# A 2x2 average pool: stores of one tile against stores of two tiles

## The chip, the cores and the metric

One core of one Trainium2 chip runs the kernel. The metric is the device time of one execution in microseconds, as a median over several runs; the profiled execution's *span* (first to last instruction) is some 1.8 us shorter. "Landing" is the moment when a DMA has signalled on all 16 engines that it is done.

## The reference

```python
# x: (32, 128, 256, 256) float32, kernel_size 2, stride 2 -> out: (32, 128, 128, 128) float32
for i in range(h_out):
    for j in range(w_out):
        output[:, :, i, j] = np.mean(x[:, :, 2*i:2*i+2, 2*j:2*j+2], axis=(2, 3))
```

1073.7 MB are read, 268.4 MB are written, each once.

## The kernel before

The output rows (32 x 128 x 128 of them, 128 floats each) are cut into tiles of 128 partitions x 32 rows. A tile's load is 64 KB per partition (8.4 MB), its store 16 KB per partition (2.1 MB). SP issues the loads, DVE adds rows and then columns, ACT multiplies by 0.25 and issues the stores. There are two input slots and two result slots in turn; a third result slot serves only the remainder at the end, which is loaded, summed and stored in pieces of 16, 8, 4 and 4 rows.

```python
    ins = [in_pool.tile([P, TILE, 2 * w], f32, name="in_tile") for _ in range(2)]
    res = [out_pool.tile([P, TILE, w_out], f32, name="res") for _ in range(3)]
    ...
    def take(engine, sem, n=1):           # wait for the semaphore, then take n off
        engine.wait_ge(sem, n)
        engine.sem_inc(sem, -n)
    def load(t, b):
        sp.dma_start(out=ins[b], in_=xt[t]).then_inc(loaded[b], 16)
    def sums(it, dst):
        dve.tensor_add(out=it[:, :, 0:w], in0=it[:, :, 0:w], in1=it[:, :, w:]).then_inc(halfway)
        take(dve, halfway)
        dve.tensor_add(out=dst, in0=it[:, :, 0:w:2], in1=it[:, :, 1:w:2]).then_inc(summed)
    def tile_sums(b):
        take(dve, stored[b], 16)          # the store of tile t-2 has landed
        take(dve, loaded[b], 16)          # the load of tile t has landed
        sums(ins[b], res[b])
    def scale_store(t, b, landed):
        take(act, summed)
        act.sem_inc(free[b])              # SP may load tile t+2
        scale(res[b])
        take(act, scaled)
        act.dma_start(out=ot[t], in_=res[b]).then_inc(landed, 16)
    ...                                   # loops over 127 whole tiles, then the pieces
```

## Time and profile before

| | before |
|---|---|
| median of the first 3 runs | 3103.62 us (3103.59 to 3103.67) |
| span of the profiled run | 3101.5 us |
| rate of all bytes over the span | 433 GB/s |
| DVE, ACT busy | 54%, 15% |

The page gives the busy share of each engine, then the two DMA queues with packets, megabytes and the share of the 16 DMA engines' time that their packets took. In the timeline a line is start, duration, engine, source line, operation, output<-input; the bracket is the idle time before it. "SPq" and "ACTq" are sequencers that issue DMAs. The lines themselves stand in the prediction.

### The profile page before, as it was taken

The numbers are of one execution on the slowest core, as the hardware profiler recorded it, in microseconds if no ns is written. First come the engines' busy times: TensorE is split into PE (matmuls) and PEld (weight loads), VectorE is DVE, ScalarE is ACT, GpSimd is POOL, SyncE is SP. The second block draws the span as 40 slices with busy tenths as digits, with TensorE's granted clock in tenths as the row PEclk, the third lists the DMA queues.
The fourth block names the chain that finished last, engine by engine and source line by source line (L and its number), as shares of the span: only waits on it lengthen the run. The fifth ranks groups of instructions, "written<-read, shape, count | busy, mean of one in ns | idle before, by whom it ended". The sixth has DMA issues, their size and how long they took to land. (4 is left out here: it accounts for less than half of the span.)

```text
span 3101.5 us, 2614 instructions
## 1 busy us (share of the span) xinstructions
DVE 1679.6 (54%) x262; ACT 464.7 (15%) x132; POOL 0.2 (0%) x4
## 2 busy tenths in 40 slices
DVE  4555555555555555555555555555555555555556
ACT  1111111111111111111111111111111111111111
POOL 0000000000000000000000000000000000000000
DMA  9999999999999999999999999999999999999999
GB/s 416 436 440 426 436 440 426 437 440 424 438 440 423 439 437 425 440 428 434 440 433 430 442 423 436 439 427 440 435 426 437 439 427 436 438 424 439 437 425 416
DMA packets 37728, 1342.19 MB, mean 433 GB/s; under 512 B 4192, under 2 KB 4192, under 8 KB 4576
## 3 DMA queue, kind: packets, MB, share of 16 engines
q1 hardware_dynamic: 19008, 1075.85, 80.1%
q10 hardware_dynamic: 18720, 266.35, 20.1%
HBM read 1073.74 MB, written 268.44 MB: 433 GB/s over the span
## 5 line engine op out<-in xcount | busy, mean ns | idle before, releaser
L87 DVE TENSOR_TENSOR in_tile<-in_tile 128x8192 f32<-128x8192 f32 (+1 forms) x131 | 1113.0, 8496 | 1396.4 <-DVEq L67 1396.4
L97 ACT ACTIVATE res<-res 128x4096 f32<-128x4096 f32 (+1 forms) x131 | 463.5, 3538 | 2594.8 <-ACTq L67 2594.8
L89 DVE TENSOR_TENSOR res<-in_tile 128x4096 f32<-128x4096 f32 (+1 forms) x131 | 566.8, 4327 | 19.2
L97 ACT ACT_TABLE_LOAD x1 | 1.3, 1283 | 36.3 <-ACTq L67 36.3
L234 POOL MEMSET const-bfloat16-1.0<- 128x1 bf16 x1 | 0.1, 101 | 0.0
L234 POOL MEMSET const-uint8-127<- 128x1 uint8 x1 | 0.1, 101 | 0.0
L234 POOL MEMSET const-float32-0.0<- 128x1 f32 x1 | 0.1, 98 | 0.2 <-issue 0.2
L234 POOL MEMSET const-float32-1.0<- 128x1 f32 x1 | 0.1, 98 | 0.0
## 6 DMA issues: line engine op xcount, KB each, us to landing
out_dram<-res ACTq DMA_DIRECT2D x126, 2048.0 KB, 30.8
in_tile<-in_x_dram SPq DMA_DIRECT2D x1, 4096.0 KB, 22.0
in_tile<-in_x_dram SPq DMA_DIRECT2D x1, 2048.0 KB, 27.1
in_tile<-in_x_dram SPq DMA_DIRECT2D x2, 1024.0 KB, 30.0
out_dram<-res SPq DMA_DIRECT2D x1, 2048.0 KB, 11.7
in_tile<-in_x_dram SPq DMA_DIRECT2D x127, 31.5
out_dram<-res ACTq DMA_DIRECT2D x1, 1024.0 KB, 8.1
out_dram<-res ACTq DMA_DIRECT2D x1, 512.0 KB, 6.0
```

The source lines that it names most:

```text
L87: dve.tensor_add(out=it[:, :, 0:w], in0=it[:, :, 0:w], in1=it[:, :, w:]).then_inc(halfway)
L89: dve.tensor_add(out=dst, in0=it[:, :, 0:w:2], in1=it[:, :, 1:w:2]).then_inc(summed)
L97: act.mul(out=dst, in_=dst, mul=0.25).then_inc(done)
L234: nc = _bacc.Bacc("TRN2", target_bir_lowering=False, num_devices=1)
```

## The change

The intent: half as many store DMAs, each twice as large. The two result slots become two pairs, ACT issues one store per pair (two 16 KB pieces per partition, which lie 2 MB apart in HBM), and DVE waits for a store only at the first tile of a pair. This takes the third slot's room, so the remainder's result goes to the input slot that no load needs any more; the remainder has three pieces (16, 8, 8).

```diff
-    res = [out_pool.tile([P, TILE, w_out], f32, name="res") for _ in range(3)]
+    both = [out_pool.tile([P, 2, TILE, w_out], f32, name="res") for _ in range(2)]
+    res = [both[t // 2][:, t % 2] for t in range(4)]
...
+    op = ov[0:2 * pairs * TILE * P].rearrange("(k t p g) f -> k p t (g f)", t=2, p=P, g=TILE)
...
-        b = rest if rest - a <= 4 else a + (rest - a) // 2
+        b = rest if rest - a <= 8 else a + (rest - a) // 2
...
-    def tile_sums(b):
-        take(dve, stored[b], 16)
-        take(dve, loaded[b], 16)
-        sums(ins[b], res[b])
+    def tile_sums(t):
+        if t % 2 == 0:
+            take(dve, stored[t // 2 % 2], 16)
+        take(dve, loaded[t % 2], 16)
+        sums(ins[t % 2], res[t % 4])
...
-    def scale_store(t, b, landed):
-        take(act, summed)
-        act.sem_inc(free[b])
-        scale(res[b])
-        take(act, scaled)
-        act.dma_start(out=ot[t], in_=res[b]).then_inc(landed, 16)
+    def scale_store(pair, c, landed):
+        for b in range(2):
+            take(act, summed)
+            act.sem_inc(free[b])
+            scale(both[c][:, b])
+        take(act, scaled, 2)
+        act.dma_start(out=op[pair], in_=both[c].rearrange("p t g f -> p t (g f)")).then_inc(landed, 16)
...
-        it, dst = ins[whole % 2], res[2]
+        it = ins[whole % 2]
+        dst = ins[(whole + 1) % 2].rearrange("p g (s f) -> p (g s) f", s=4)[:, 0:TILE]
...                                       (loops regrouped to match; last waits adapted)
```

## The prediction

Passages that no trace or run of this case shows are cut from the prediction and from some expectations, at the marks. No term of the sum is among them: it stands as 3103.62 - 0.65 + 0.7 = 3103.7.

> **What bounds the kernel now.** I read the page first: busy shares, slices, DMA queues.
>
> ```profile
> span 3101.5 us, 2614 instructions
> DVE 1679.6 (54%) x262; ACT 464.7 (15%) x132; POOL 0.2 (0%) x4
> DMA  9999999999999999999999999999999999999999
> ...
> DMA packets 37728, 1342.19 MB, mean 433 GB/s; under 512 B 4192, under 2 KB 4192, under 8 KB 4576
> ...
> q1 hardware_dynamic: 19008, 1075.85, 80.1%
> q10 hardware_dynamic: 18720, 266.35, 20.1%
> ```
>
> No compute engine is near its limit; the 16 DMA engines are busy in every slice. q1 (loads, issued by SP) and q10 (stores, issued by ACT) take 80.1 + 20.1 = 100.2% of the engines' time: they are full, and packets even overlap a little. The bytes are given: 1073.7 MB in, 268.4 MB out. The chain of waits at the page's end tells nothing here (only the last scale is in it), so I went to the timeline, in the middle of the run:
>
> ```profile
> 1510.36 72.93 SPq L84 DMA_DIRECT2D in_tile<-in_x_dram  x4
> 1514.04 0.34 ACTq L104 DMA_DIRECT2D out_dram<-res  x1
> 1520.94 8.69 DVE L87 TENSOR_TENSOR in_tile<-in_tile 128x8192 f32<-128x8192 f32 x1 [10.93 <-DVEq L67]
> 1529.78 4.43 DVE L89 TENSOR_TENSOR res<-in_tile 128x4096 f32<-128x4096 f32 x1
> 1534.39 3.62 ACT L97 ACTIVATE res<-res 128x4096 f32<-128x4096 f32 x1 [20.58 <-ACTq L67]
> 1538.24 0.34 ACTq L104 DMA_DIRECT2D out_dram<-res  x1
> 1545.13 8.69 DVE L87 TENSOR_TENSOR in_tile<-in_tile 128x8192 f32<-128x8192 f32 x1 [10.93 <-DVEq L67]
> ```
>
> A tile takes 1545.13 - 1520.94 = 24.19 us, for 8.389 MB in and 2.097 MB out: 433.5 GB/s, the mean of the whole run. DVE needs 13.3 us of it and waits 10.9. What ends that wait is to be seen from the landings of the two issuing lines, loads first, then stores:
>
> ```profile
> DMA to landing us min/median/max: 21.8/31.5/40.7
> ...
> DMA to landing us min/median/max: 19.5/30.8/33.8
> ```
>
> The load issued at 1510.36 lands at about 1541.9; the store issued at 1514.04 lands at 1514.04 + 30.8 = 1544.8, and DVE starts at 1545.13. So DVE starts at the landing of the *store* of two tiles earlier, and the load lay ready for 3 us. This looks as if the store buffers bound the kernel, and is the trap of this profile: the store is slow only because the engines are full. When one store lands, the next is already queued (issued at 1538.24), and so is the next load (issued at about 1534.5). Neither queue runs dry, so an earlier start of DVE would only lengthen a queue.
>
> The last view is the DMA view of two short windows, from 24 to 34 us (loads alone) and from 1508 to 1520 us (both):
>
> ```profile
> q1 hardware_dynamic: 64, 4.19, 96.7%
> ...
> q1 hardware_dynamic: 80, 4.19, 80.7%
> q10 hardware_dynamic: 79, 1.05, 20.5%
> ```
>
> 64 load packets in 96.7% of 16 x 10 us are 2.42 us each, for 64 KB. In the second window 64 load packets and 16 tiny ones that end a load take 80.7% of 16 x 12 us; the window before it has the 64 alone at 80.6%. So the 16 tiny ones of a whole DMA cost 0.1% of 192 us, 0.2 us in all or about 0.01 us on each engine (rounding allows 0 to 0.02). The stores' 64 packets of 16 KB and 15 tiny ones come to 39.4 us: 0.61 us a packet, a quarter of a load packet. Large and small packets have the same rate here, with stores or without.
>
> [...]in that window the two queues show 64 packets each of data, and thus 4 bytes loaded per byte stored, just what the kernel needs.[...] Here partitions stay 16 KB apart; only the two pieces of one partition lie 2 MB apart. Nothing in the trace of before tests that.
>
> **The change, part by part.**
>
> *Fewer stores.* Before: 126 + 1 + 4 = 131 stores. After: 63 pairs, tile 126 alone, and three pieces (16, 8, 8) of the rest: 67. One piece fewer is loaded too. So 65 DMAs go, each with one tiny packet per engine: 65 x 0.01 = 0.65 us, at most 1.3. The data packets remain 64 KB and 16 KB, so the data time stays. The 64 issues (0.34 us each) and waits saved on ACT lie in its 20 us of idle time per tile: 0.
>
> *Buffers of four tiles in two pairs.* A pair is stored after its second tile, so tile 2k+4 waits for a store issued in tile 2k+1, three tiles earlier, and not two. Follow one turn from the landing of the older pair at T. DVE starts the even tile, and its input is free at T+13.5. The odd tile's load lands about 23 us after T and its pair is issued at T+23+17.3 = T+40. The younger pair lands at T+48.4 (16 packets at one per 2.42+0.61 us). So when it lands the next has been queued for 8 us, and at T+13.5 the odd tile's load still has some 9 us to go: neither queue runs dry, and the period stays 48.4 us for two tiles. Saving 0, loss 0. What moves is latency: a pair lands 96.8 - 40 = 56 us after its issue, and even tiles wait for the store, odd ones for the load.
>
> *The start.* The first store goes out after tile 1 (about 59.5 us) and not at 41.36. Loads fill the engines meanwhile, because the loads of tiles 2 and 3 are issued when tiles 0 and 1 are summed: 0. Loads are ahead by about 8 more packets per engine for the rest of the run, so tile 126 starts some 8 x 0.61 = 5 us earlier, near 3062.5 instead of 3067.57. This is no gain, as the same 4 MB of stores are then still to do.
>
> *The end.* The first packets move at about 1.9 us, the last at 3099.1 (27 GB/s in the slice from 3099, none later). At 433.5 GB/s the bytes need 3096.2 us of these 3097.2. So before has 1 us of holes, and a better end can give 1 us at most. After: about 14 us of loads and stores of the rest still compete with a 4 MB pair, so the second piece lands near 23 us after the start of tile 126 and not at 18, the third near 29. Its two sums (2.29 + 1.23), scale (1.06) and issue end near 35, its store starts near 36.5 and carries 8 rows, not 4. Other stores (tile 126 with 4.9 us, the first two pieces) fill the engines to about 36. So the hole is small: 0 to 2 us lost, taken as 0.7. Writing the result over an input tile costs nothing[...].
>
> Sum: 3103.62 - 0.65 + 0.7 = 3103.7; I predict **3103.6 us**.
>
> **The rivals.**
> (a) *DVE's store wait was the bound*, and more slack removes it: 3 us per tile x 127 = 380 us, giving 2720 us. For it: the wait's end. Against: 1342.19 MB in 2720 us is 493 GB/s, above anything that the profile shows over several packets.
> (b) *A fixed cost per DMA* is hidden in the gaps[...]. The tiny packets' share speaks against it.
> (c) *Pairs starve a queue*: the store queue empties for some us per pair while loads wait for DVE. Losing 1 us per pair makes 3167. Against: 8 and 9 us of margin, and loads alone keep the engines full (96.7%, or 433 GB/s by the packet time).
> (d) *Two write streams 2 MB apart slow down in HBM.* If a store packet took 0.7 instead of 0.61, 128 x 8 x 0.09 = 92 us would be added: 3196. Only the chip can tell.
> (e) *The end costs more*: if the last piece waits for a pair that drains late, 3 to 4 us: 3107.
>
> **Range and chances.** Bytes and rate fix all but about 1 us of gain, so below 3101 would need (b). Above, (e) reaches 3107. Range 3101 to 3107.5. Over 2% faster would need 442 GB/s throughout: 0.01. Over 2% slower needs (c) or (d) in earnest: 0.03. Within 2%: 0.96.
>
> **What would show it.** Right: DMA at 433 GB/s; q1 and q10 shares within 0.3 of 80.1% and 20.1%; about 1040 fewer packets under 512 B; pairs of tiles every 48.4 us with starts alternately closer and farther apart than 24.19; stores landing near 56 us; tile 126 starting near 3062. Wrong: a store share above 20.5% (rival d), slices under 9 of DMA or a pair period above 48.6 (c)[...]; a last load or store with idle engines before it beyond 2 us (e).

## The result, and the profile after

After takes 3103.16 us (median of 6 runs, 3103.09 to 3103.29), before 3103.61 us in the same job (6 runs, 3102.92 to 3103.67). A ratio here is the mean time of one kernel's runs over that of the other's of the same rounds, so not quite the ratio of the medians: 0.9999, with a 95% interval from 0.9986 to 1.0012. A difference of 0.45 us is inside the interval. Executions over 1.5% slower than the fastest of the same kernel are left out of the means. Both profiled spans are 3101.5 us.

The page of after, busy shares and queues:

```profile
span 3101.5 us, 2136 instructions
DVE 1679.6 (54%) x260; ACT 464.5 (15%) x131; POOL 0.2 (0%) x4
...
DMA packets 36432, 1342.19 MB, mean 433 GB/s; under 512 B 3152, under 2 KB 3152, under 8 KB 3408
...
q1 hardware_dynamic: 18864, 1075.85, 80.1%
q10 hardware_dynamic: 17568, 266.34, 20.0%
```

The 65 DMAs that went took 4192 - 3152 = 1040 tiny packets with them, 16 each. Loads have the same share of engine time, stores 0.1 points less.

The timeline of after in mid-run (loads of SP, pair stores of ACT, and the starts of DVE):

```profile
1504.91 97.04 SPq L87 DMA_DIRECT2D in_tile<-in_x_dram  x5
1508.60 0.38 ACTq L109 DMA_DIRECT2D out_dram<-res  x1
1514.87 8.69 DVE L90 TENSOR_TENSOR in_tile<-in_tile 128x8192 f32<-128x8192 f32 x1 [10.31 <-DVEq L69]
...
1539.65 8.69 DVE L90 TENSOR_TENSOR in_tile<-in_tile 128x8192 f32<-128x8192 f32 x1 [11.51 <-DVEq L69]
...
1556.96 0.38 ACTq L109 DMA_DIRECT2D out_dram<-res  x1
1563.23 8.69 DVE L90 TENSOR_TENSOR in_tile<-in_tile 128x8192 f32<-128x8192 f32 x1 [10.32 <-DVEq L69]
```

and the landings of the two issuing lines, loads first, then pair stores:

```profile
DMA to landing us min/median/max: 21.8/34.6/40.7
...
DMA to landing us min/median/max: 28.6/52.3/53.9
```

Two tiles take 1563.23 - 1514.87 = 48.36 us; before they took 48.38. What DVE waits for has changed: the load issued at 1504.91 lands at 1504.91 + 34.6 = 1539.5 and DVE starts at 1539.65. The store issued at 1508.60 lands at 1508.60 + 52.3 = 1560.9, and the tile that may use its slot starts at 1563.23. Every tile now starts at the landing of a *load*; the store lies landed for 2 us. The semaphore times of the whole trace say the same: from tile 4 to 124, DVE starts 0.14 us after its load's landing in after, and 0.25 us after its store's in before.

Over the steady part the period is (3044.59 - 117.85)/121 = 24.188 us per tile before and (3038.70 - 136.71)/120 = 24.183 us after: 0.005 us less, or 0.6 us over 126 tiles. The starts in after are 24.78 and 23.58 us apart by turns, with the longer gap behind the even tile.

The ends, in the timelines (start of tile 126, first sum of the last piece, last store). Before:

```profile
3067.57 8.69 DVE L87 TENSOR_TENSOR in_tile<-in_tile 128x8192 f32<-128x8192 f32 x1 [9.71 <-DVEq L67]
...
3093.08 1.22 DVE L87 TENSOR_TENSOR in_tile<-in_tile 128x1024 f32<-128x1024 f32 x1
...
3095.98 0.34 ACTq L154 DMA_DIRECT2D out_dram<-res  x1
```

After:

```profile
3062.27 8.69 DVE L90 TENSOR_TENSOR in_tile<-in_tile 128x8192 f32<-128x8192 f32 x1 [10.31 <-DVEq L69]
...
3091.13 2.29 DVE L90 TENSOR_TENSOR in_tile<-in_tile 128x2048 f32<-128x2048 f32 x1 [1.53 <-DVEq L69]
...
3096.07 0.34 ACTq L159 DMA_DIRECT2D out_dram<-in_tile  x1
```

Tile 126 starts 5.3 us earlier, yet the last store is issued within 0.1 us of where it was. The stretch between has become longer because the same bytes were still to be moved.

### The profile page after: what moved, and what is told of

It is laid out like the page before. It is cut to its first block, busy times and chain, and to the rows that moved or that the text cites. A ratio compares the mean times of both kernels' runs of the same rounds, so it can differ in the third digit from the quotient of the medians.

```text
span 3101.5 us, 2136 instructions
## 1 busy us (share of the span) xinstructions
DVE 1679.6 (54%) x260; ACT 464.5 (15%) x131; POOL 0.2 (0%) x4
## 2 busy tenths in 40 slices
DMA packets 36432, 1342.19 MB, mean 433 GB/s; under 512 B 3152, under 2 KB 3152, under 8 KB 3408
## 3 DMA queue, kind: packets, MB, share of 16 engines
q1 hardware_dynamic: 18864, 1075.85, 80.1%
## 5 line engine op out<-in xcount | busy, mean ns | idle before, releaser
L101 ACT ACTIVATE res<-res 128x4096 f32<-128x4096 f32 x127 | 459.2, 3616 | 2582.4 <-ACTq L69 2582.4
L92 DVE TENSOR_TENSOR res<-in_tile 128x4096 f32<-128x4096 f32 x127 | 561.9, 4425 | 18.6
## 6 DMA issues: line engine op xcount, KB each, us to landing
out_dram<-res ACTq DMA_DIRECT2D x63, 4096.0 KB, 52.3
in_tile<-in_x_dram SPq DMA_DIRECT2D x127, 34.6
```

Of the source, the lines that this page charges most:

```text
L101: act.mul(out=dst, in_=dst, mul=0.25).then_inc(done)
```

## The experiments

Twelve kernels ran, all with the right result. Each is timed against before on the same chip; the median of before was 3103.55 in the first job, 3103.42 in the second and 3103.51 in the third.

For some of them I read the trace's packet records, one per packet with queue, start, duration and size. They don't name the engine; I took a packet to be on the engine whose last packet had just ended. L is a load's data packet, S a store's; "L." and "S." are the 4-byte packets that end a load or a store on this engine. One engine each, some 50 us, in mid-run:

```
before           L S L. S L S. L S L S L S L S L S L S L. S L S. L S L S L S L S L S L S L. S L S. L
after            S L. S L S L S L S L S L S L S. L L L. L S L S L S L S L S L S L S L S L. S L S L S
one_piece        L. L S. L L L L L L L L. L L[2856] S L[2906] S L S L S L S L S L S L. S L S. L L L L
one_piece_split  L S. L S L S L S L S L S L S L S L. S L S. L S L S L S L S L S L S L S L. S L S. L S
```

(The number in brackets is a packet's ns where it is over 2500; in these rows the other data packets of loads are 2418, and a 16 KB store packet is 611.) In these rows the queues take strict turns, one packet each (before, 1496 to 1508 us: 64 load packets and 65 of stores), and **the 4-byte packet takes a turn of its own**. Before has 8 + 1 = 9 turns for a load and 9 for a store. After has 18 turns for two loads and 17 for a pair, and so once per pair there is no store packet to put between two loads: from the fourth pair on, the pair before has ended on 10 to 15 of the 16 engines when the next is issued.

**1. Was DVE's wait for the store the bound?** The kernel before, with its three result slots in turn:

```diff
-        take(dve, stored[b], 16)          # b = t % 2
+        take(dve, stored[t % 3], 16)
-        sums(ins[b], res[b])
+        sums(ins[t % 2], res[t % 3])
```

> The kernel before with its three result tiles taken in turn, so that tile t waits for the store of tile t-3 and not t-2; the rest's result goes to the free input tile. All transfers keep their sizes. Engines-full theory (the 16 DMA engines' packet times set the time): same time as before within 1 us, 3102.6 to 3104.6; DVE then starts at the landing of a load, and each store lies landed long before it is asked for; tiles stay 24.2 us apart. Store-wait theory (DVE's wait for the store set the pace): clearly faster, by some 3 us per tile, 2720 us at the extreme, and at the very least below 3090.

3104.01 us (3103.78 to 3104.08), ratio 1.0001 [0.9988, 1.0014]. Stores from 33.9 us issue to landing, loads 34.6:

```profile
out_dram<-res ACTq DMA_DIRECT2D x126, 2048.0 KB, 33.9
...
in_tile<-in_x_dram SPq DMA_DIRECT2D x127, 34.6
```

A load now takes 34.6 us where it took 31.5. The freed wait turned into a longer queue, as the engines-full theory has it. Rival (a) has fallen; the 493 GB/s that it needed are above every slice of the page of before (442 at most).

**2. What does a DMA more cost?** Before, with each whole store issued as two stores of 64 partitions (same packets, 126 more DMAs):

```diff
-        act.dma_start(out=ot[t], in_=res[b]).then_inc(landed, 16)
+        for h in range(2):
+            half = slice(h * P // 2, (h + 1) * P // 2)
+            act.dma_start(out=ot[t][half], in_=res[b][half]).then_inc(landed, 16)
```

> The kernel before with 126 stores each issued as two stores of 64 partitions: 126 more DMAs, the same 16 KB data packets. Packet theory (a DMA costs an engine only the tiny packet that ends it, 0.009 us in the trace's packet records): 126 x 0.009 = 1.1 us more, 3104.0 to 3106.[...]

3228.27 us (3222.77 to 3241.93), ratio 1.0407. The packet theory did not have this. Load packets lengthened: their mean in the packet records is 2519 ns and not 2419, which over 1016 packets per engine is 101 of the 125 us. The store packets hardly changed (614 ns on average, 611 before). The records show stretches of "S S S S." without a load, in which the load queue stands empty, and after them the first loads are long. Run 5 returns to it.

**3. Smaller pieces as well.** Before, with each whole store as two stores of 16 rows (8 KB packets):

```diff
+        for h in range(2):
+            half = slice(h * TILE // 2, (h + 1) * TILE // 2)
+            act.dma_start(out=ot[t][:, half], in_=res[b][:, half]).then_inc(landed, 16)
```

> The kernel before with 126 stores each issued as two stores of 16 rows: 126 more DMAs as in the run with halves of the partitions, but data packets of 8 KB too. Packet theory: two packets of 8 KB take 2 x 0.309 us where one of 16 KB took 0.611 (both seen in the trace, the small ones at its end), so 8 x 126 x 0.007 = 7 us, plus the 1.1 us of the endings: 3111 to 3113. Fixed-cost theory, in which only the number of DMAs counts: the same as with halves of the partitions[...]. A danger for both: with turns of one packet each the store queue gets half of its former share, so that DVE may wait for stores while the load queue runs dry; then it is longer, above 3120, with slices of DMA below 9.

3880.9 us (3875.84 to 3883.84), ratio 1.2503. The danger named there came true. In the view of stretches (DVE, ACT, POOL busy, clock, DMA share, GB/s), the stretch in which two waiting tiles are summed at last:

```profile
1546.00:1560.00 14.00, 13.28 (x3) 0.00 (x0) 0.00 (x0) 1.00 0.26 111
```

A store now needs 18 turns and a load 9. Stores fall behind, both loads lie landed, DVE waits for a store, and when it goes on the DMA engines have little to do. Whole-run DMA shares are 66.3% and 16.3%, together 83%.

**4. Larger pieces.** After, with 64 neighbouring rows per partition and pair, so that a pair leaves as one 32 KB piece per partition:

```diff
-    xt = xv[...].rearrange("(t p g) f -> t p g f", p=P, g=TILE)
-    op = ov[...].rearrange("(k t p g) f -> k p t (g f)", t=2, p=P, g=TILE)
+    xt = xv[...].rearrange("(k p t g) f -> k t p g f", t=2, p=P, g=TILE)
+    op = ov[...].rearrange("(k p u) f -> k p (u f)", p=P, u=2 * TILE)
```

> The kernel after with the rows dealt out otherwise: a partition has 64 neighbouring rows of a pair, so that a pair's store is one 32 KB piece per partition and the whole store is 4 MB in a row; loads keep 64 KB packets. The number of DMAs is that of after. Packet theory: 8 packets of 1.213 us take the place of 16 of 0.611 on each engine, 0.072 us per pair, 63 x 0.072 = 4.5 us less than after: 3098 to 3099.5. Fixed-cost theory: no change, 3103.2. If two pieces 2 MB apart in HBM had cost anything, more than 4.5 us would be gained.

3166.03 us (3151.68 to 3186.76), ratio 1.0205 [1.0178, 1.0231]: slower where 4.5 us were to be gained. (The interval lies across the 2% mark, so the recorded verdict is "unclear"; that the kernel is slower than before is not in doubt, as its fastest run is 48 us above.) The page:

```profile
span 3169.0 us, 2136 instructions
...
q1 hardware_dynamic: 18864, 1075.85, 80.5%
q10 hardware_dynamic: 9504, 266.34, 19.5%
```

80.5% of 3169.0 us is 2551 us per engine for the same load packets that took 80.1% of 3101.5 = 2484 us in after: 67 us more. The store packets did get cheaper: 19.5% of 3169.0 = 618 against 620 us, and in the packet records, which have no rounding, 617.3 against 621.5, 4.2 us. The DMA view of one-piece from 1545 to 1550 us, when a new store has just begun, shows where the 67 us arise:

```profile
q1 hardware_dynamic: 17, 1.11, 59.5%
```

17 load packets in 59.5% of 16 x 5 us are 2.80 us each, not 2.42 (up to 4.0 in the records). By what mechanism they lengthen is not shown. The records' row above shows the setting: a pair needs 8 + 1 turns, half of what the loads of its period need, so the store queue is empty for half the load turns, and the load packets around its new start are the long ones. That the empty queue is to blame, and not the loads' pieces lying 128 KB apart in HBM, was still open; run 6 tells them apart.

**5. Balance the turns again.** Before, with loads and stores both halved, once by partitions and once by rows (the store edits of runs 2 and 3, and the same `half` in the load):

```diff
-        sp.dma_start(out=ins[b], in_=xt[t]).then_inc(loaded[b], 16)
+            sp.dma_start(out=ins[b][half], in_=xt[t][half]).then_inc(loaded[b], 16)
# or        sp.dma_start(out=ins[b][:, half], in_=xt[t][:, half]).then_inc(loaded[b], 16)
```

By rows:

> The kernel before with every whole load and every whole store issued as two DMAs of 16 rows: packets of 32 KB and 8 KB, 18 turns to 18 per tile. Turn theory: balance is back, and a tile costs each engine 16 x 1.213 + 16 x 0.309 + 4 x 0.009 us where it was 8 x 2.418 + 8 x 0.611 + 2 x 0.009: 0.14 us more, 17 us over 126 tiles: 3118 to 3124, against 3881 where the stores alone were halved. Rival, that stores of 8 KB pieces are slow in themselves: 3880 or more.

3113.6 us (3113.39 to 3113.9), ratio 1.0033 [1.0020, 1.0046]. With 18 turns to 18, the 777 us that halved stores cost are down to 10. The same 8 KB packets and even more DMAs are there; the balance made the difference. The 10 us are less than the 17 expected: per tile 24.268 - 24.188 = 0.080 us for 16 more data packets and 2 more tiny ones, 4 to 5 ns a packet, because packets overlap somewhat (in before, an engine's packets add up to 3105.8 us in some 3097, 3.7 ns each). It also caps what a DMA can cost an engine: if all 0.080 us were due to the two extra DMAs, 0.04 us each.

By partitions:

> The kernel before with every whole load and every whole store issued as two DMAs of 64 partitions: 252 more DMAs, data packets as before. Turn theory: each engine gives the two queues turns of one packet, and the 4-byte packet that ends a DMA takes a turn too; before has 9 turns for a load and 9 for a store, the halved stores alone had 9 to 10 and fell behind, here it is 10 to 10 and the balance is back: 3103.6 + 253 x 0.009 = 3106, 3104 to 3109. Rival, that stores of 64 partitions themselves, or so many DMAs, cost the 125 us: 3228 or more.

5536.63 us (5521.26 to 5575.6), ratio 1.7845. Here the turn theory was wrong. Of its rival's two forms the number of DMAs is out, as the halves by rows have as many (3113.6 us); what is left is that a DMA of 64 partitions is slow in itself. The page:

```profile
span 5573.8 us, 3363 instructions
...
q1 hardware_dynamic: 21040, 1075.86, 85.9%
q10 hardware_dynamic: 20736, 266.35, 14.1%
```

85.9% of 5573.8 us is 4788 us per engine for 1016 load packets of 64 KB and the remainder, so about 4.7 us each, twice 2.42. The stores took 14.1%, 786 us where they took 622; their packets are 771 ns on average in the records. The factor of two is the loads' alone: store packets are a quarter longer here, and in run 2, where the loads had all 128 partitions, hardly at all (614 ns). Why loads of 64 partitions have packets twice as long is not shown. So run 2 says nothing clean of what a DMA costs, nor of turns. Its loss lies in load packets behind an empty load queue; whether the 10 to 9 turns or the halved stores emptied that queue stays open.

**6. One-piece's layout with balanced turns.** As run 4, but a pair leaves as two DMAs of 16 KB per partition:

```diff
+        for b in range(2):
+            act.dma_start(out=op[pair][:, b], in_=both[c][:, b].rearrange("p g f -> p (g f)")).then_inc(landed, 16)
```

> The kernel with 64 neighbouring rows per partition and pair (loads of 64 KB pieces that lie 128 KB apart in HBM), but a pair is stored by two DMAs issued one after the other, 16 KB per partition each. Turn theory: the one-piece kernel lost 63 us because its 32 KB pieces drain at twice the load queue's proportion and the store queue then stands empty for a third of each period, and load packets lengthen when it starts again; with 18 turns to 18 for two tiles the loss is gone: 3102.5 to 3105, load packets 2.42 us. Rival, the loads' pieces 128 KB apart: still about 3166.

3104.04 us (3103.72 to 3104.36), ratio 1.0002 [0.9988, 1.0015]; load packets are 2418 ns again (mean 2419). The loads' layout is cleared; the size and turns of the stores made run 4 slow. This run also shows the pattern that the prediction had expected of after. Its timeline:

```profile
1516.48 8.69 DVE L91 TENSOR_TENSOR in_tile<-in_tile 128x8192 f32<-128x8192 f32 x1 [14.08 <-DVEq L69]
...
1537.52 8.69 DVE L91 TENSOR_TENSOR in_tile<-in_tile 128x8192 f32<-128x8192 f32 x1 [7.77 <-DVEq L69]
...
1564.84 8.69 DVE L91 TENSOR_TENSOR in_tile<-in_tile 128x8192 f32<-128x8192 f32 x1 [14.06 <-DVEq L69]
```

and its stores' landings:

```profile
DMA to landing us min/median/max: 22.5/34.0/57.7
```

Starts are 21.0 and 27.3 us apart by turns. The later half of a pair, issued at about 1506.9, lands some 57.7 us later at 1564.6, and DVE starts at 1564.84: with 18 turns for the stores the first tile of a pair does wait for its store.

**7. How much margin is there?** After, with the second sum repeated once, then twice, in tiles 0 to 123 (same result, more DVE work):

```diff
+            for _ in range(again):        # again = 1, 2
+                take(dve, halfway)
+                dve.tensor_add(out=res[t % 4], in0=it[:, :, 0:w:2], in1=it[:, :, 1:w:2]).then_inc(halfway)
```

> The kernel after with the second sum done twice in tiles 0 to 123 (4.6 us more DVE work per tile, same result). Engines-full theory: the next load is issued 4.6 us later but still some 5 us before the load under way has landed; stores come later too, and even tiles then wait for them, but in a loop of four tiles of 92 us against 96.7: 3103 to 3107. If the landing, or DVE after it, paced the kernel: 124 x 4.6 = 570 us more, 3670.

3104.34 us (3104.05 to 3105.93), ratio 1.0004 [0.9991, 1.0017]. 549 us more of DVE work (2228.3 us busy, not 1679.6) cost about 1 us. DVE does not pace the kernel.

> The kernel after with the second sum done three times in tiles 0 to 123: 9.1 us more DVE work per tile, 22.4 us of a period of 24.2, so DVE would still have time. Margin theory: the loop from a pair's issue over its landing (52.3 us) to the second tile after it and its own issue is now some 101 us against 96.7, and loads are issued as the last one lands: the margin is used up, 1 to 6% slower, 3130 to 3280, with load packets above 2.42 us or slices of DMA below 9. If only DVE's busy time mattered: 3103 to 3107.

3208.84 us (3207.11 to 3216.44), ratio 1.0352 [1.0339, 1.0365]. The next 4.6 us per tile cost 105 us, though DVE is still only 87% busy. The page:

```profile
q1 hardware_dynamic: 18864, 1075.85, 79.6%
q10 hardware_dynamic: 17568, 266.34, 19.4%
```

Load packets took 79.6% of 3205.3 = 2551 us per engine, again 67 us more than in after, and the records show stretches of stores alone and of loads alone in turn. The other 37 us are time in which the engines were not full: with the stores' 19.4%, the two queues fill 99.0% of the span and not 100.1%.

**8. One pair slot.** After, with a single pair of result tiles, so that the margin is gone altogether:

```diff
-    both = [... for _ in range(2)]
+    both = [... for _ in range(1)]
-            take(dve, stored[t // 2 % 2], 16)
+            take(dve, stored[0], 16)
```

> The kernel after with one pair of result tiles in place of two: the even tile waits for the store of the pair just before. Margin theory: the store is issued about 31 us after the even tile's start, shares the engines with the two loads issued before it and lands about 66 us after that start, while the engines run out of work at the end of each turn: about 66 us per pair in place of 48.4, 4100 to 4450 in all, DMA slices at 7 to 8. If DVE's waits for stores did not matter at all: 3103.

4198.83 us (4196.82 to 4200.14), ratio 1.3529 [1.3508, 1.3550]. In the stretch in which the first tile of a pair is summed, the DMA share is zero:

```profile
1537.00:1550.00 13.00, 12.85 (x3) 0.00 (x0) 0.00 (x0) 1.00 0.00 0
```

The pair period is 1602.24 - 1536.78 = 65.5 us (66 expected). Pairs need the second slot.

**9. The end.** After with the pieces 16, 8, 4, 4 and before with 16, 8, 8 (one number each: the 8 in the condition becomes 4, the 4 becomes 8).

> The kernel after with the last pieces of before (16, 8, 4, 4 rows in place of 16, 8, 8). Engines-full theory: the end of after has at most 1 us of holes, the last piece is ready about 1 us sooner, and one more DMA is issued: 3102.3 to 3103.3, between 0 and 0.9 us faster than after. If the end of after had cost as much as 3 us[...]: about 3100.

3103.63 us (3103.49 to 3103.68), ratio 1.0000 [0.9987, 1.0014]. That is 0.1 us above before in the same job, and 0.5 us above after's median of another job, not up to 0.9 below.

> The kernel before with the last pieces of after (16, 8, 8). Engines-full theory: 0 to 1.5 us slower than before, 3103.5 to 3105, as the last 8 rows are summed, scaled and stored in one go behind the last load. If the end of after had cost 3 us: 3106.5.

3103.39 us (3103.19 to 3104.62), ratio 1.0001 [0.9987, 1.0014]. The expected small loss doesn't show either. How the last rows are cut makes no difference that these runs resolve.

No experiment beat both kernels by more than the noise. What is left above the bytes is small: 3096 us at 433.5 GB/s, 1.9 us before the first packet, some 2.4 us after the last.

## Why the prediction was right

The time, 3103.16, is 0.44 us from the predicted 3103.6.

- **Engines full, waits harmless:** right, and shown by runs 1 and 7 (3104.01 and, with the second sum done twice, 3104.34 us). DVE's wait for a store was a symptom of full queues.
- **Fewer stores, 0.65 us:** the tiny packets went as counted (1040). The steady period fell by 0.005 us per tile, 0.6 us in all, which fits, but a difference that small is not resolved in the times. Rival (b), a cost per DMA, is bounded: run 5 by rows caps it at 0.04 us, and the period of after at about 0.02 (0.005 us for half a DMA less per tile, give or take the 0.006 us per tile by which before's own runs differ).
- **Neither queue runs dry, rival (c):** right for the time and for the loads, wrong for the stores. The pair that lands was to find the next one queued for 8 us; in the records most engines have finished the older pair before the next is issued (at 1555.6 to 1555.9 us on 12 of 16, the issue at 1556.96). The store queue stands empty for about one turn per pair. That this cost nothing was luck, as far as the prediction goes: load packets are 2419 ns on average as before, but in one-piece, with a longer gap, they lengthened (2.80 us in the stretch of run 4). There the loss was 63 us in 63 pairs, by chance just the 1 us per pair that (c) had assumed, though with the engines busy all the time; with one pair slot it was 1095 us, 17 per pair.
- **Even tiles wait for the store, stores land near 56 us:** wrong. All tiles wait for loads and stores land after 52.3 us. The step that failed counted 16 packets of a pair against 16 of its two loads and left out that the 4-byte packets take turns too, one for the pair and two for the loads. With 17 turns to 18 the stores gain on the loads until the store is no longer what comes last; run 6, with 18 to 18, shows the predicted pattern (57.7 us). The sign "starts alternately closer and farther apart" did come, but the other way round: predicted were some 23 us from the even to the odd tile, measured are 24.78 (run 6: 21.0).
- **The start, tile 126 near 3062.5:** 3062.27. Bytes postponed are still to be moved, and the last store was issued 0.1 us later than in before.
- **The end, second piece 23 us and third 29 us after tile 126:** 23.7 (3085.93) and 28.9. The 0.7 us for a hole are neither confirmed nor refuted; run 9 found nothing in either direction. Writing over an input tile did cost nothing: a second sum of 128x1024 took 1.22 to 1.23 us there, 1.23 in the result slot of before.
- **Rival (d), pieces 2 MB apart in HBM:** fallen. The stores' share is 20.0%, and their packets are 611 ns as before.

## What to carry to other kernels

When the DMA engines are full in steady state, halving the number of transfers was worth no more here than the packets that end them (0.65 us counted, 0.6 over the steady part); look at what an engine's queues hold, not at which wait ended last. Where two queues share the engines, count turns: pieces per transfer plus one, for loads and for stores. A balance of turns (9 to 9, 18 to 17) kept both kernels at 433 GB/s, while larger store pieces (32 KB) cost 2% and smaller ones (8 KB, beside loads of 64 KB) 25%, although each seems harmless by itself; and keep a transfer on all 128 partitions: with loads and stores on 64 the load packets took about 4.7 us in place of 2.42, and the kernel 5536.63 us.
